# A decoder trunk on one core: the engine that forms the modulation values

## The chip, the core and the metric

The kernel runs on one NeuronCore of a Trainium2 chip. Five engines work beside each other from their own instruction queues: TensorE (PE, matrix products into PSUM), VectorE (DVE), ScalarE (ACT), GpSimd (POOL) and SyncE (SP, which here only issues loads). 16 DMA engines move data between HBM and SBUF. The metric is the device time of one execution in microseconds; lower is better.

## The reference

The program is a trunk of two layers over 256 tokens of 1024 features. Each layer is steered by a conditioning vector `c`:

```python
c_act = silu(c)
for l in range(2):
    mod = (c_act @ ada_w[l] + ada_b[l]).reshape(bsz, 6, 1, 1024)
    shift1, scale1, gate1, shift2, scale2, gate2 = (mod[:, i] for i in range(6))
    h = rmsnorm(x, mix_norm_g[l]) * (1 + scale1) + shift1
    # four mixers of h: S5, sparse attention, RG-LRU, RWKV-7; their gated merge; a projection
    x = x + gate1 * mixed
    h2 = rmsnorm(x, ffn_norm_g[l]) * (1 + scale2) + shift2
    x = x + gate2 * moe(h2, ...)      # 16 experts, 2 of them per token
```

`mod` is a product of one row with a matrix of 1024 x 6144 per layer: little arithmetic, and 25 MB of float32 weights per layer that are read once.

## The kernel before

All weights come in pages of [128, 2048] float32 (1 MB) over SP's queue, in one order that is fixed when the program is built (`order`, line 173 on). A page goes to one of five ring pages; where the state `wide` is set (line 1666, after the mixers), it may also go to one of 15 general pages as long as more than `keep` of them are free (`issue`, `ahead`). A page is given back by `done`, which at once issues the next load that finds room.

The 6144 modulation values of a layer are three groups of 2048 (shift1 and scale1; gate1 and shift2; scale2 and gate2). A group's weights are eight pages, one for each 128 of the 1024 conditioning features; `ada(l, g, kt)` (line 447) takes one of them. Its output are four rows of 512, at partitions 0, 32, 64 and 96. There are two ways:

- Groups (0, 0) and (1, 0), named by `EARLY` (line 26), use PE: per page four matmuls of 32 columns by 512 (line 460), which accumulate in one PSUM bank `acc` over the eight pages. The trace has two records for each float32 matmul. Such a set of four is called a pack here.
- The other four groups use DVE: each page is multiplied by its feature's `csil` and added to a partial sum of [128, 2048] in a general page, in four instructions of 512 columns (line 468; the first page by ACT, line 466). After the eighth page a pack of PE with a matrix of ones sums over the partitions (line 474).

Then both add the bias (line 476), and `mod_values` transposes and stores the values.

Group (0, 0) is needed first and runs at the start, before anything else on PE. The others are among the work of `fill` (line 1262), which lies beside the mixers: `fill_plan` puts two or three pages of modulation weights ahead of each gate product (`feat_steps`, line 614: 48 products of 128 x 128 x 256 per page, in three parts of 12 significant bits that ACT and DVE form, lines 581 and 582). Layer 0 has groups (0, 1), (0, 2) and (1, 0) there, layer 1 has (1, 1) and (1, 2). The main loop steps three chains (RWKV; attention, then S5, then RG-LRU; the tables of S5) in turn, and `fill` by one to three steps for each round of them. This gives the order in which the program is written. The framework then sets, at build time and by its own cost estimate, the order of each engine's queue: an operation that is ready may go ahead of an earlier one that is not. On the chip each engine's order is fixed. Tiles of PSUM have tags with a number of banks: `acc` three, `mx` two, `rw` three.

Of the kernel before, what the change touches and what calls it, by code (L numbers as in the profile page):

```python
"""Hybrid decoder trunk: S5, sparse attention, RG-LRU and RWKV-7 mixers, gated merge, grouped MoE."""
# [13 lines left out]
F32R = mybir.dt.float32r                 # 12 significant bits: a float32 is exactly the sum of two  # L15
AF = mybir.ActivationFunctionType
OP = mybir.AluOpType
# [8 lines left out]
EARLY = [(0, 0), (1, 0)]                 # modulation values by PE instead of DVE: layer, group  # L26
NW = 2                                   # buffers of halves of weights
NR, NM = 5, 15                           # pages of 8 KB per partition: of the weight stream, of everything else
KEEP = 1                                 # pages of the latter that the stream leaves free
FILL, SPARE = (2, 2, 2, 2, 1, 3, 3), 2   # work beside the mixers: steps of it per step of them, pages it leaves free  # L30
XAT, MAT_AT = 3, 3                       # pages of the stream that x and the small matrices follow
PLAN = "1311330100b0322d22ac"            # that work: gates of a branch (0 to 3), its merge (a to d)
PSB = dict(acc=3, mx=2, rw=3)            # banks of PSUM: dense products, small ones, RWKV
TM = (164, 256, 256, 256)                # columns of iq | ik | iw, of q, k and v
# [5 lines left out]
# Columns of the per-feature parameters of a layer: name, number of columns.  # L40
# [9 lines left out]
# Small matrices of a layer, side by side.  # L50
# [27 lines left out]
class Pages:  # L78
    """Pages of [128, 2048] float32 in SBUF, whole or in slots of 512; the longest free goes first."""

    def __init__(self, pool, name, n):
        self.tiles = [pool.tile([P, 2048], F32, tag=f"{name}{i}", name=f"{name}{i}") for i in range(n)]
        self.free_pages = list(range(n))
        self.slots = []                 # free slots of split pages: (page, slot)
        self.used = {}                  # page -> slots in use, of split pages
        self.owner = {}
# [60 lines left out]
def _emit(ctx, tc, I, out):  # L147
# [26 lines left out]
    # ------------------------------------------------------------------ weight stream  # L174
    order, loaded = [], {}
    state = dict(next=0, wide=False)

    def fill_plan(l):
        """What runs beside the mixers: the gates, and modulation values that are needed later."""
        groups = [(l, 1), (l, 2)] + ([(l + 1, 0)] if l + 1 < L else [])  # L180
        adas = [("ada", ll, g, kt) for ll, g in groups for kt in range(KT)]
        plan, k, ng, seen = [], 0, len(groups), [0] * 4
        for c in PLAN:
            if c.isdigit():
                plan += adas[k:k + ng] + [("gate", l, seen[int(c)], int(c))]
                k += ng
                seen[int(c)] += 1
            else:
                plan.append(("br", l, "abcd".index(c)))
        return plan  # L190
# [41 lines left out]
    def ahead():  # L232
        while state["next"] < len(order):
            key = order[state["next"]][0]
            if state["wide"] and key[0] not in ("br", "out", "w13", "w2", "gate", "ada"):
                state["wide"] = False
# [14 lines left out]
    # ------------------------------------------------------------------ inputs and constants  # L251
# [45 lines left out]
    # Masks of 64 x 64 tiles: rows (p mod 64) are s, columns t; t > s, t >= s, and the blocks that  # L297
    # the recursive inverse joins.
# [17 lines left out]
    # Slots of a pair (e, e + 8) of experts: 32..95 and then 0..31 for e, 96..127 and then 0..31 for e + 8.  # L316
# [3 lines left out]
    # Of four, an earlier one (last index) also goes before an equal one.  # L320
# [8 lines left out]
    # ------------------------------------------------------------------ small accurate functions  # L329
# [22 lines left out]
    def sincos(sn, cs, ang, shape):  # L352
        """Reduction by quarter turns in parts that multiply exactly, then polynomials."""
# [26 lines left out]
        half(y, n)                                                       # floor(n / 2)  # L380
        V.scalar_tensor_tensor(m, y, -2.0, n, op0=OP.mult, op1=OP.add)   # n mod 2
        half(n, y)
        V.scalar_tensor_tensor(y, n, -2.0, y, op0=OP.mult, op1=OP.add)
        V.tensor_scalar(y, y, -2.0, 1.0, op0=OP.mult, op1=OP.add)        # sign
# [11 lines left out]
    def exp_acc(o, a, shape):  # L396
        """exp to about a unit in the last place; zero where it underflows."""
# [22 lines left out]
    def log1p_twice(o, q, t, s):  # L420
        """2 log(1 + q) for q in 0..1, by an atanh series."""
        V.tensor_scalar(o, q, 2.0, None, op0=OP.add)
        V.reciprocal(o, o)
        V.tensor_tensor(o, o, q, OP.mult)                                # at most 1 / 3
# [9 lines left out]
    # ------------------------------------------------------------------ conditioning  # L434
# [12 lines left out]
    def ada(l, g, kt):  # L447
        """Of 2048 of the 6144 modulation values, one of 8 parts of the sum; they end in rows
        0, 32, 64, 96 of [128, 512]."""
        early = (l, g) in EARLY  # L450
        if kt == 0:
# [3 lines left out]
            part[l, g] = b, pt("acc", [P, 512]) if early else M.take([P, 2048])  # L455
        b, p = part[l, g]
        w = get(("ada", l, g, kt))
        if early:
            for j in range(4):
                PE.matmul(p[32 * j:32 * j + 32, :], csil[:, kt, :], w[:, 512 * j:512 * j + 512],  # L460
                          start=kt == 0, stop=kt == KT - 1)
        else:
            for j in range(4):
                js = slice(512 * j, 512 * j + 512)
                if kt == 0:
                    S.activation(p[:, js], w[:, js], AF.Copy, scale=csil[:, kt, 0:1])
                else:
                    V.scalar_tensor_tensor(p[:, js], w[:, js], csil[:, kt, 0:1], p[:, js], op0=OP.mult, op1=OP.add)  # L468
        done(("ada", l, g, kt))
        if kt == KT - 1:  # L470
            if not early:
                a, p = p, pt("acc", [P, 512])
                for j in range(4):
                    PE.matmul(p[32 * j:32 * j + 32, :], ones_f[:, 0:32], a[:, 512 * j:512 * j + 512], start=True, stop=True)
                M.free(a)
# [3 lines left out]
    def ada_cols(r):  # L479
        """[128, 4, 4]: value j * 512 + c * 128 + p of the group."""  # L480
# [7 lines left out]
    def ada_rows(o, r, j0):  # L488
        """Half of rows j0, j0 + 1 of the group on every partition, [128, 1024]."""
# [34 lines left out]
    def gate_rows(l, i):  # L524
        """Half of gate i (0 of the mixers, 1 of the experts) on every partition."""
# [6 lines left out]
    # ------------------------------------------------------------------ norm  # L532
# [5 lines left out]
    def rstd(ss, a):  # L538
        """1 / norm of the tokens of a tile."""
# [16 lines left out]
    def modT(x, rs, sc, sh, put):  # L556
        """Feature-major normalised and modulated input: put(k2, p, f) takes blocks 2 k2 and 2 k2 + 1,
        f(kt, o, p) is the modulation of one."""
# [20 lines left out]
    def halves(hi, lo, a):  # L579
        """a is hi + lo, each of 12 bits."""  # L580
# [12 lines left out]
    def hs(h, kt, a=None):  # L593
        """A block of features of the input, of all tokens or of a half."""
        return h[:, T * kt:T * kt + T] if a is None else h[:, T * kt + P * a:T * kt + P * a + P]

    def chunks(key, n):
        """The halves of a page of weights, four blocks of n columns at a time: (kt, hi, lo)."""
# [8 lines left out]
    def three(p, kt, wh, wl, first, last, a=None):  # L607
        """p += weights times input, without the product of the low halves. The first and the last of a bank
        are told: its columns are one group."""
# [8 lines left out]
    def feat_steps(p, key, nb):  # L618
        """nb blocks of 128 features, feature-major: [128, nb, 256]."""
# [15 lines left out]
    # ------------------------------------------------------------------ tables  # L635
# [15 lines left out]
    def prep():  # L651
        sh, s3 = [P, NS], [P, L, 8]
        lre, lim, a, b, sn, cs = (sm(f"s5p{k}", s3, F32, 1) for k in range(6))
        # exponentials of log_step and, for softplus(-lam) = max(-lam, 0) + log(1 + exp(-|lam|)), of -|lam|
# [16 lines left out]
        # (lam_bar - 1) / lam  # L671
# [28 lines left out]
    def s5_tables(l, tabs):  # L700
        """cos and sin of t * theta, [128, 8, 256] each, by doubling."""
# [32 lines left out]
    def others(l, m, tabs, brs):  # L734
        """The other three mixers one after another, their projections first."""
# [13 lines left out]
    # ------------------------------------------------------------------ RWKV-7  # L749
# [11 lines left out]
    def rwkv(l, m, brs):  # L761
# [46 lines left out]
        # decay = exp(-exp(-1/2) sigmoid(z)) = (1 - T) / (1 + T)  # L808
# [13 lines left out]
        # the key's direction, normalised per head  # L822
# [55 lines left out]
        # products of pairs of tokens, transposed: [s, chunk, {t > s, t >= s}, t]  # L878
# [16 lines left out]
        # X = (I + A)^-1 by doubling the block, and Y = X^T  # L895
# [38 lines left out]
        # chunks in turn  # L934
# [41 lines left out]
        # norm over the head  # L976
# [22 lines left out]
    # ------------------------------------------------------------------ sparse attention  # L999
# [23 lines left out]
    def dsa(l, o, brs):  # L1023
# [35 lines left out]
        for a in range(2):  # L1059
            n = P * (a + 1)  # L1060
            ta = slice(P * a, P * a + P)
            # indexer
# [17 lines left out]
            # the 64 largest, the first of equals before the others  # L1080
# [52 lines left out]
    # ------------------------------------------------------------------ S5  # L1133
    def gelu2(o, y):
        """2 * gelu(y)."""
# [8 lines left out]
    def s5(l, u, m, tabs, brs):  # L1144
        cs, sn = tabs
        # C times (lam_bar - 1) / lam
# [15 lines left out]
        for blk in range(2):  # L1162
# [20 lines left out]
            # Re(C s): s_re = cos w_re - sin w_im, s_im = cos w_im + sin w_re  # L1183
# [32 lines left out]
    # ------------------------------------------------------------------ RG-LRU  # L1216
# [574 lines left out]
```

## Time and profile before

| | |
|---|---|
| timed runs | 1261.24, 1261.74, 1262.14 us; median 1261.74 |
| the profiled execution, first to last instruction | 1258.4 us |
| PE busy | 1105.5 us (88%) |
| DVE busy | 752.8 us (60%) |
| ACT busy | 374.1 us (30%) |
| POOL busy | 257.5 us (20%) |
| data read from HBM | 327.19 MB |

The profiled execution's own time is that span; the page gives none beside it. Busy means that at least one instruction of the engine was under way. The ends of matmuls are modelled, so that successive products overlap in the record. The mixers take about 44 to 346 us in layer 0 and 661 to 944 us in layer 1, the experts 400 to 607 and 1000 to 1250 us. A granted clock of 1.00 is 2.4 GHz, and 1.2 GHz is the other level; a value between is the mean over a stretch.

### The profile page before, as it was taken

How to read it: one execution, taken by the hardware profiler on the slowest of the kernel's cores; microseconds unless marked ns; L12 is line 12 of the kernel's file. 1: busy time of each engine (PE TensorE's matmuls, PEld its weight loads, DVE VectorE, ACT ScalarE, POOL GpSimd, SP SyncE). 2: the span in 40 equal slices, each digit the busy share in tenths (PEclk: the TensorE clock that was granted, in tenths of full speed). 3: DMA queues.
4: the chain of work that ended last, by engine and by line, in shares of the span. 5: the costliest groups of instructions: out<-in, count | busy, mean ns of one | idle time of the engine just before them, and what ended most of it. 6: DMA issues, size and time to landing. Idle time of an engine off the chain costs nothing. (4 is left out here: it accounts for less than half of the span.)

```text
span 1258.4 us, 22758 instructions
## 1 busy us (share of the span) xinstructions
PE 1105.5 (88%) x9286; PEld 722.1 (57%) x9286; DVE 752.8 (60%) x1439; ACT 374.1 (30%) x662; POOL 257.5 (20%) x320
## 2 busy tenths in 40 slices
PE   3878999988986999998849899998898699999894
PEld 0878886856873345332218798886677444443321
DVE  5789995598666134232275899959877623233223
ACT  1543433415432111110026544541354211011101
POOL 0593112151232000000091111115414200000000
PEclk8888999989997999998969899999899799999897
DMA  9635787625564999999803468832346489999951
GB/s 357 232 126 208 294 304 292 244 70 199 179 255 150 362 407 421 421 421 410 323 34 134 137 235 299 302 135 101 140 177 255 165 323 416 421 420 420 419 223 52
DMA packets 47089, 329.83 MB, mean 262 GB/s; under 512 B 5992, under 2 KB 6120, under 8 KB 7552
## 3 DMA queue, kind: packets, MB, share of 16 engines
q1 hardware_dynamic: 45776, 327.47, 66.9%
q8 instruction: 78, 1.28, 0.4%
q10 hardware_dynamic: 1200, 0.79, 0.2%
q14 instruction: 35, 0.29, 0.1%
HBM read 327.19 MB, written 1.05 MB: 261 GB/s over the span
## 5 line engine op out<-in xcount | busy, mean ns | idle before, releaser
L614 PE MATMUL acc<-h_hi,whi 128*128 128x256 f32 x720 | 213.8, 297 | 0.2 <-ACT whi L581 0.2
L614 PE MATMUL acc<-h_hi,wlo 128*128 128x256 f32 x720 | 206.3, 287 | 3.5 <-DVE wlo L582 3.5
L614 PE MATMUL acc<-h_lo,whi 128*128 128x256 f32 x720 | 206.4, 287 | 3.3 <-DVE h_lo L582 3.3
L582 DVE TENSOR_TENSOR wlo<-ring,whi 128x1024 fp32r<-128x1024 f32 (+2 forms) x122 | 152.6, 1254 | 62.7 <-ACT whi L581 54.7
L581 ACT ACTIVATE whi<-ring 128x1024 fp32r<-128x1024 f32 (+2 forms) x122 | 125.9, 1033 | 208.9 <-PE acc L614 145.9
L1560 PE MATMUL acc<-page,page 128*32 128x512 f32 (+1 forms) x1408 | 174.3, 600 | 0.0
L614 PEld LDWEIGHTS acc<-h_hi,whi 128*128 128x128 f32 x720 | 138.6, 192 | 16.8 <-issue 7.4
L614 PEld LDWEIGHTS acc<-h_lo,whi 128*128 128x128 f32 x720 | 139.0, 193 | 7.4 <-DVE h_lo L582 4.1
L614 PEld LDWEIGHTS acc<-h_hi,wlo 128*128 128x128 f32 x720 | 139.0, 193 | 6.7 <-DVE wlo L582 4.5
L1560 PEld LDWEIGHTS acc<-page,page 128*32 128x32 f32 x1408 | 48.8, 110 | 95.2 <-issue 90.8
L1591 DVE SCALAR_TENSOR_TENSOR page<-mx,moslw,page 128x512 f32<-128x512 f32 x32 | 24.0, 751 | 124.9 <-PE mx L1584 124.9
L1584 PE MATMUL mx<-page,page 128*32 (+1 forms) x704 | 87.4, 630 | 5.2 <-ACT page L1485 5.2
L1560 PE MATMUL acc<-ring,page 128*32 128x512 f32 (+1 forms) x640 | 84.7, 595 | 0.0
L468 DVE SCALAR_TENSOR_TENSOR page<-ring,csil,page 128x512 f32<-128x512 f32 x112 | 83.0, 780 | 0.0
L1516 POOL TENSOR_TENSOR page<-page,page 128x512 f32<-128x512 f32 x6 | 7.6, 1271 | 328.4 <-DVE page L1515 233.2
L1538 DVE TENSOR_TENSOR page<-page,acc 128x512 f32<-128x512 f32 x64 | 41.7, 683 | 51.9 <-PE acc L1537 51.2
L1474 DVE SCALAR_TENSOR_TENSOR page<-page,acc 128x512 f32<-128x512 f32 x16 | 11.0, 687 | 96.9 <-ACT page L1473 96.9
L1584 PEld LDWEIGHTS mx<-page,page 128*32 128x32 f32 x704 | 24.1, 116 | 59.3 <-issue 49.1
L581 ACT ACTIVATE wlo<-page 128x512 fp32r<-128x512 f32 x32 | 20.2, 631 | 123.5 <-DVE page L1591 123.5
L1473 ACT ACTIVATE page<-acc 128x512 f32<-128x512 f32 x16 | 9.6, 597 | 154.2 <-PE acc L1560 154.2
L1317 POOL TENSOR_TENSOR page<-page,page 128x512 f32<-128x512 f32 x21 | 32.3, 1557 | 79.3 <-DVE page L1315 78.3
L1537 PE MATMUL acc<-wlo,whi 128*128 128x512 f32 x128 | 44.7, 438 | 2.3 <-ACT wlo L581 1.4
(514 smaller groups left out, 2102.8 us busy)
## 6 DMA issues: line engine op xcount, KB each, us to landing
page<-in_w SPq DMA_DIRECT2D x132, 1024.0 KB, 12.1
ring<-in_w SPq DMA_DIRECT2D x60, 1024.0 KB, 11.3
ring<-in_ada_w SPq DMA_DIRECT2D x48, 1024.0 KB, 5.2
ring<-in_gate_w SPq DMA_DIRECT2D x32, 1024.0 KB, 5.8
ring<-in_branch_w SPq DMA_DIRECT2D x8, 1024.0 KB, 4.8
ring<-in_w_rw SPq DMA_DIRECT2D x6, 1024.0 KB, 10.2
ring<-in_w_tm SPq DMA_DIRECT2D x6, 1024.0 KB, 4.8
ring<-in_w_fm SPq DMA_DIRECT2D x6, 1024.0 KB, 4.8
```

The lines of the kernel that those rows point to most:

```text
L468: V.scalar_tensor_tensor(p[:, js], w[:, js], csil[:, kt, 0:1], p[:, js], op0=OP.mult, op1=OP.add)
L581: S.activation(hi, a, AF.Copy)
L582: V.tensor_tensor(lo, a, hi.bitcast(F32), OP.subtract)
L614: PE.matmul(p, w, x_, **f)
L1317: G.tensor_tensor(mix[dp], mix[dp], t, OP.add)
L1473: S.activation(a, h1, AF.Tanh, scale=0.5)
L1474: V.scalar_tensor_tensor(b, a, 1.0, h1, op0=OP.add, op1=OP.mult)
L1537: PE.matmul(p, oh[:, P * a:P * a + P], y[:, fs], start=y is yh, stop=y is yl)
L1538: V.tensor_tensor(x[:, a, fs], x[:, a, fs], p, OP.add)
L1560: PE.matmul(hh[f][32 * g:32 * g + 32, :], xg[:, kt, P * i + 32 * g:P * i + 32 * g + 32], w[:, ds(offs[g] + 512 * f, 512)], start=kt == 0, ...
L1584: PE.matmul(yp[f][32 * g:32 * g + 32, :], gT[:, ft, 32 * g:32 * g + 32], w[:, ds(offs[g] + 512 * f, 512)], start=ft == 0, stop=ft == 3)
L1591: V.scalar_tensor_tensor(t, yp[f], now["w"][:, i:i + 1], gate2[:, fs], op0=OP.mult, op1=OP.mult)
```

## The change

All six groups go the way of `EARLY`: the branch, the partial sum in a general page and the pack with ones are gone, and each group holds one bank of `acc` from its first page to its last. The state `wide` is set from the beginning, with eight general pages kept free, and the load of `x` no longer ends it; so the last three pages of group (0, 0) may go to general pages, until the first weights of RWKV end it. Comments are taken out too, which shifts the line numbers by a few.

```diff
-EARLY = [(0, 0), (1, 0)]
...
-    state = dict(next=0, wide=False)
+    state = dict(next=0, wide=True, keep=8)
...
-            if state["wide"] and key[0] not in ("br", "out", "w13", "w2", "gate", "ada"):
+            if state["wide"] and key[0] not in ("br", "out", "w13", "w2", "gate", "ada", "x"):
                 state["wide"] = False
...
     def ada(l, g, kt):
-        early = (l, g) in EARLY
         if kt == 0:
             b = M.take([P, 512])
             G.memset(b, 0.0)
             nc.scalar.dma_start(b[0:P:32, :], I["ada_b"][l, g])
-            part[l, g] = b, pt("acc", [P, 512]) if early else M.take([P, 2048])
+            part[l, g] = b, pt("acc", [P, 512])
         b, p = part[l, g]
         w = get(("ada", l, g, kt))
-        if early:
-            for j in range(4):
-                PE.matmul(p[32 * j:32 * j + 32, :], csil[:, kt, :], w[:, 512 * j:512 * j + 512],
-                          start=kt == 0, stop=kt == KT - 1)
-        else:
-            for j in range(4):
-                js = slice(512 * j, 512 * j + 512)
-                if kt == 0:
-                    S.activation(p[:, js], w[:, js], AF.Copy, scale=csil[:, kt, 0:1])
-                else:
-                    V.scalar_tensor_tensor(p[:, js], w[:, js], csil[:, kt, 0:1], p[:, js], op0=OP.mult, op1=OP.add)
+        for j in range(4):
+            PE.matmul(p[32 * j:32 * j + 32, :], csil[:, kt, :], w[:, 512 * j:512 * j + 512],
+                      start=kt == 0, stop=kt == KT - 1)
         done(("ada", l, g, kt))
         if kt == KT - 1:
-            if not early:
-                a, p = p, pt("acc", [P, 512])
-                for j in range(4):
-                    PE.matmul(p[32 * j:32 * j + 32, :], ones_f[:, 0:32], a[:, 512 * j:512 * j + 512], start=True, stop=True)
-                M.free(a)
             V.tensor_tensor(b, p, b, OP.add)
             mod_values(l, g, b)
```

## Rows read from the trace of the kernel before

**Rows 1.** The page's part 1: busy us, share of the span, instructions.

```profile
PE 1105.5 (88%) x9286; PEld 722.1 (57%) x9286; DVE 752.8 (60%) x1439; ACT 374.1 (30%) x662; POOL 257.5 (20%) x320
```

**Rows 2.** Windows, layer 0's mixers: length; PE, PEld, DVE, ACT, POOL busy; PE clock; DMA share; GB/s.

```profile
94.00:126.00 32.00, 27.43 (x215) 25.72 (x216) 29.55 (x46) 12.42 (x16) 12.77 (x14) 0.89 0.56 207
126.00:158.00 32.00, 30.71 (x443) 27.03 (x442) 31.31 (x60) 15.39 (x31) 5.83 (x5) 1.00 0.78 294
158.00:189.00 31.00, 29.53 (x478) 26.90 (x477) 29.23 (x53) 11.70 (x27) 3.22 (x2) 1.00 0.84 303
189.00:221.00 32.00, 31.04 (x326) 21.79 (x319) 19.14 (x44) 10.45 (x22) 6.90 (x9) 1.00 0.77 292
...
252.00:284.00 32.00, 29.15 (x172) 19.34 (x173) 31.12 (x47) 3.86 (x6) 16.61 (x17) 0.89 0.23 78
...
sum 252.00, PE 232.78 PEld 194.56 DVE 202.14 ACT 98.59 POOL 62.91; mean PE 29.10 PEld 24.32 DVE 25.27 ACT 12.32 POOL 7.86
```

**Rows 3.** The same windows over layer 1's mixers.

```profile
724.00:755.00 31.00, 31.00 (x351) 28.99 (x351) 28.80 (x42) 13.56 (x23) 5.64 (x5) 1.00 0.66 237
...
787.00:818.00 31.00, 31.00 (x411) 27.81 (x409) 29.62 (x53) 16.27 (x38) 3.36 (x3) 1.00 0.83 307
...
sum 252.00, PE 234.59 PEld 204.18 DVE 212.72 ACT 107.90 POOL 57.19; mean PE 29.32 PEld 25.52 DVE 26.59 ACT 13.49 POOL 7.15
```

**Rows 4.** Line 468: durations in ns, first and last start; its busy time in eight windows.

```profile
L468 DVE SCALAR_TENSOR_TENSOR page<-ring,csil,page x112: 714/741/1695, 109.0 to 809.2; 128x512 f32<-128x512 f32 x112
...
sum 253.00, DVE 83.04; mean DVE 10.38
```

**Rows 5.** Order of time on PE around packs: start us, busy us, operation.

```profile
151.32 1.06 PE L474 MATMUL acc<-page,ones_f 128*32 128x512 f32 x8
152.31 0.39 PE L614 MATMUL acc<-h_hi,whi 128*128 128x256 f32 x1
...
193.65 1.06 PE L460 MATMUL acc<-ring,csil 128*32 128x512 f32 x8
...
204.65 2.78 PE L460 MATMUL acc<-ring,csil 128*32 128x512 f32 x24
207.36 0.38 PE L614 MATMUL acc<-h_hi,whi 128*128 128x256 f32 x1
207.58 0.28 PE L614 MATMUL acc<-h_lo,whi 128*128 128x256 f32 x1
```

**Rows 6.** PE's holes: one in order of time; then waits, 246 to 346 us (total, times, longest).

```profile
97.72 1.12 PE L842 MATMUL rw<-identr,page 128*128 128x128 f32 x4 [4.77 <-DVE page L837]
...
PEld mx L1186 <- POOL page L1179: 7.1, 4, 2.9
...
PE mx L1186 <- DVE page L1178: 5.6, 3, 2.7
```

**Rows 7.** The start: a wait of PE, loads that SP issues, windows as in rows 2.

```profile
PE acc L460 <- DMA ring<-in_ada_w: 5.8, 4, 3.2
...
8.24 9.74 SPq L228 DMA_DIRECT2D ring<-in_ada_w  x4
...
0.00:8.00 8.00, 0.00 (x0) 0.00 (x0) 2.71 (x32) 1.49 (x2) 2.40 (x17) 1.00 0.60 177
8.00:16.00 8.00, 3.27 (x16) 0.80 (x20) 7.69 (x73) 0.00 (x0) 0.00 (x0) 1.00 0.99 408
...
24.00:32.00 8.00, 5.74 (x25) 0.75 (x26) 1.82 (x6) 1.04 (x2) 0.00 (x0) 0.59 1.02 422
```

**Rows 8.** Order of time on DVE: the search's rounds with and without sums.

```profile
149.02 0.28 DVE L1083 MAX8 dsm<-page 128x8 f32<-128x128 f32 x1
...
150.79 0.28 DVE L1083 MAX8 dsm<-page 128x8 f32<-128x128 f32 x1
...
202.34 0.43 DVE L1083 MAX8 dsm<-page 128x8 f32<-128x256 f32 x1
...
203.32 0.43 DVE L1083 MAX8 dsm<-page 128x8 f32<-128x256 f32 x1
```

## The prediction

> **What bounds the kernel now.** I read the page's busy line first, then a table of equal windows over the two mixer stretches, then the waits of TensorE (PE) in them, then the order of time around the operations that the change moves. The busy line puts PE at 1105.5 of 1258.4 us and VectorE (DVE) at 752.8 [rows 1]: PE is the busiest engine over the whole, but that is a mean over stages. The table is the view that decides. Where the modulation sums run on DVE, in layer 0 from 109.0 us on [rows 4] and in layer 1 up to 809, both engines look full: DVE 31.31 of 32 and 29.23 of 31 us, PE 30.71 of 32 and 29.53 of 31 [rows 2], and in layer 1 PE 31.00 of 31 [rows 3]. So which of the two sets the pace? Three things say PE. In the window right behind, 189 to 221, DVE has no such sums and falls to 19.14 of 32, yet PE stays at 31.04 of 32 at full clock [rows 2]: freeing DVE did not free PE. Between 85 and 252 us PE has only one long wait, 4.77 us on L837, and it ends at 97.72 us [rows 6], before the first sum on DVE. And what DVE does in the sums is filler: no instruction is listed as waiting for L468, and only the end of a group has a reader. So in these stretches PE works through a list that is always full, and DVE is full beside it because it was given filler.
>
> **The change part by part.**
>
> *Added on PE.* Four groups of eight pages, so 32 packs of four matmuls of 32 columns each. Group (1, 0) already runs this way beside the mixers of layer 0, so the price is measured in place: three packs take 2.78 us, 0.93 each, and one alone 1.06 [rows 5]. I take 0.93: 32 x 0.93 = 29.8 us, and 33.9 at the upper end.
>
> *Removed from PE.* Each of the four groups ended with a pack that summed over partitions (L474). It begins at 151.32 and the next product at 152.31 [rows 5]: 0.99 us, so 4 x 0.99 = 4.0 us. Net on PE: +25.8 us.
>
> *Removed from DVE and ACT.* 112 instructions of L468, 83.0 us of DVE [rows 4], and eight activations a layer on ACT, which is far from full. I cost this at nothing: PE covers it, since PE does not wait there for DVE. If that cover were not there it would be worth up to 83 us; the first rival below is about that.
>
> *What PE's holes give back.* PE is idle 252.0 - 232.8 = 19.2 us between 94 and 346 and 252.0 - 234.6 = 17.4 us between 692 and 944 [rows 2, 3]. The 4.77 us hole at L837 can take packs if their pages are there: three, 2.8 us. The other large holes belong to the S5 mixer (7.1 and 5.6 us on L1179 and L1178 [rows 6]); PE's order is fixed when the program is built and it stands in that order behind a product that waits, so more filler does not fill them by itself. I take 4 us for all others in both layers together. Ends: nothing, or all 36.6.
>
> *Tile shape.* A pack works in 32 columns between products of 128. The first product after three packs took 0.38 us, the next 0.28 [rows 5]: 0.10 us for the way back. Many packs stand beside 64-column products of RWKV, which change the shape anyway, so I take 0; the upper end is 32 x 0.10 = 3.2 us. The Trainium skill, TensorEngine Tiling (Array Packing), Key Properties, says that changing the tiling mode drains TensorE; this is the rule that speaks against the change. The trace agrees with it by those 0.10 us; counted on the way in and the way out, 64 x 0.10 = 6.4 us, it would make the forecast 1287 instead of 1281.
>
> *The bank.* A group now keeps one of three accumulator banks for its eight pages, and products of the gates have two. Group (1, 0) does that in 189 to 221, and PE is idle 0.96 us there [rows 2], no more than beside it. I take 0; the upper end is that whole idle time for each of four groups, 3.8 us. The first pack of a group waits for a free bank and the fill's later products stand behind it on PE, until ACT has read one of the gates' banks.
>
> *Big pages at first.* The last three pages of group (0, 0) go to the general pages at once instead of waiting for ring pages. But the DMA engines are busy 0.99 to 1.02 of the time in the windows from 8 to 32 us [rows 7], of which the first and the last of three are shown: the bytes that come before the last of these pages are the same, so it lands no sooner. The first 8 us have idle DMA time, but there the issue of later pages was behind (the fifth page goes out at 8.24 us [rows 7]) while ring pages were free. What could be gained is that gap, (1 - 0.60) x 8 = 3.2 us [rows 7]; what could be lost, by small loads that come later behind more large ones, I bound by the 3.2 us longest wait of PE for a modulation page [rows 7]. I take 0. On the queue of SyncE the weights of RWKV stay behind the eight pages and x, in the same order; on GpSimd and ACT the clearing and the bias load of a group stay where they are.
>
> *Pages.* A group no longer holds a page of 8 KB per partition for its partial sums, so the stream and the fill may find a page sooner; with PE full that is worth 0, and the bound is within the holes above.
>
> *Sum.* 25.8 - 2.8 - 4 = +19 us on the profiled execution: 1258.4 to about 1277.4. The timed runs have their median at 1261.74, 3.3 us over that span, which I leave as it is: 1261.7 + 19 = **1281**. What is late next is everything behind the packs on PE: the mixers' products, then the merge, the output projection, and the expert stage, which starts that much later in each layer and has its own load stream tied to the same pages.
>
> **The rivals.**
>
> *DVE was the limiter (faster).* Mechanism: the mixers' chains wait on DVE's in-order queue behind the sums. The top-64 search shows it: in layer 0 its rounds begin at 149.02 and 150.79, 1.77 us apart with sums between, and at 202.34 and 203.32, 0.98 apart without, although each step is longer there [rows 8]. Chains that end earlier let S5 start earlier and leave more gate products to lie beside it. Against it: PE was not waiting for those chains. Price: it decides from the point where more than 25.8 of PE's 36.6 idle us come back; if all do, -10.8, that is **1251**. The Trainium skill, Perfetto Trace Analysis, Identifying the Most-Contended Engine, says that matmul busy time is no good measure for TensorE and that the busy share of weight loads is better. By that, PE is 27.03 / 32 = 84% and 26.90 / 31 = 87% full where I call it full [rows 2], and this rival has more room than I give it; that no wait is seen there keeps me with the other.
>
> *It comes out even.* The holes, the cold clock (0.89 granted in 94 to 126 and in 252 to 284 [rows 2], so 3.5 us lost in each, PE being less busy there) and the earlier chains return just about the 25.8: **1262**.
>
> *Dearer.* Packs at 1.06, the way back at 0.10, the bank's 3.8, no hole filled: 33.9 - 4.0 + 3.2 + 3.8 = +36.9, **1299**.
>
> *It does not do what it says.* The big pages may never matter, since the ring is not what limits the start; that is my value for that part, and it changes nothing in the sum.
>
> **How the numbers follow.** PE-bound with part of the holes, 0.60: between +13 (another 6 us of holes back) and +27 (no hole filled, a little for the way back), 1275 to 1289, likeliest 1281. DVE the limiter, 0.18, 1251. Even, 0.09. Dearer, 0.13. Runs of this kernel lie within 0.9 us, and 0.2% (2.5 us) is about what can be told from no change. Faster is the second case, 0.18; same the third, 0.09; slower the first and the fourth, 0.73. The range must take in the even case, a part of the faster one and the lower part of the dearer one: 1256 to 1292.
>
> **What would show it.** Right: the packs of L460 are three times as many as before, DVE busy falls by about 80 us, and PE busy rises by 20 to 28 us; in the windows that hold the packs PE stays above 95% while DVE falls towards 60%; the start of layer 0's expert stage and of layer 1 move later by about 10 us each; the last pack of group (0, 0) begins within 1 us of where it did. Wrong: PE's busy time rises but the stretch of mixers gets shorter, with S5 starting earlier; or PE shows waits on the loads of modulation pages or on the reading of a bank; or the first product of layer 0 comes some us earlier.

## The result, and the profile after

The changed kernel takes 1275.92 us (median of 4 runs, 1272.37 to 1279.4) where the kernel before took 1261.49 (4 runs, 1257.71 to 1262.14): the ratio is 1.0119 with a 95% interval of 1.0091 to 1.0148. It is slower by about 14 us; the forecast was 1281, 19 over before. The profiled execution has a span of 1273.4 us against 1258.4, 15.0 more.

Lines behind the modulation code have moved: L460 of before is L457, L614 is L599, L842 is L827, L1083 is L1068, L1483 is L1468, L1560 is L1545, L1576 is L1561 and L1584 is L1569.

The page's part 1 and its group of the packs from ring pages (instructions, busy us, mean ns), and then, from the view of that line, the packs that read general pages:

```profile
PE 1129.7 (89%) x9510; PEld 729.8 (57%) x9510; DVE 678.2 (53%) x1327; ACT 364.5 (29%) x646; POOL 250.6 (20%) x320
...
L457 PE MATMUL acc<-ring,csil 128*32 128x512 f32 x360 | 47.0, 618 | 16.5 <-DVE csil L439 12.6
```

```profile
L457 PE MATMUL acc<-page,csil x24: 1061/1062/1063, 24.1 to 30.1; 128*32 128x512 f32 x24
```

PE is 24.2 us busier than in [rows 1], DVE 74.6 less busy, and there are 360 + 24 = 384 records of packs, three times 128.

The windows of layer 0's mixers, with the columns of [rows 2]:

```profile
126.00:158.00 32.00, 32.00 (x440) 25.18 (x443) 14.29 (x38) 11.81 (x27) 4.94 (x6) 1.00 0.72 280
158.00:189.00 31.00, 30.59 (x446) 23.15 (x440) 12.33 (x19) 10.29 (x24) 1.22 (x2) 1.00 0.73 281
189.00:221.00 32.00, 31.31 (x333) 22.18 (x329) 17.16 (x38) 9.40 (x19) 5.67 (x8) 1.00 0.72 280
221.00:252.00 31.00, 31.00 (x335) 25.67 (x336) 13.36 (x26) 13.27 (x31) 0.29 (x1) 1.00 0.71 281
```

From 126 to 189 us DVE has fallen from 60.54 us [rows 2] to 26.62, less than half of the 63 us. PE is as full as it was and passes fewer instructions: 886 matmul records where it passed 921. That is the whole case in two numbers: the engine that was relieved was not the one that set the pace.

Where the 15.0 us arise is read from four marks, the starts of single operations in the order of time on PE: the first product of the RWKV norm and the first of the expert stage, in each layer. Of before:

```profile
400.41 1.08 PE L1560 MATMUL acc<-page,page 128*32 x4
...
711.93 0.60 PE L842 MATMUL rw<-identr,page 128*128 128x128 f32 x4
...
1005.19 1.08 PE L1560 MATMUL acc<-page,page 128*32 x4
```

(its first mark, 97.72, is in [rows 6]), and of the changed kernel:

```profile
99.28 1.12 PE L827 MATMUL rw<-identr,page 128*128 128x128 f32 x4 [3.60 <-DVE page L822]
...
413.00 1.08 PE L1545 MATMUL acc<-page,page 128*32 x4
...
721.12 0.60 PE L827 MATMUL rw<-identr,page 128*128 128x128 f32 x4
...
1024.42 1.08 PE L1545 MATMUL acc<-page,page 128*32 x4
```

The marks are later by 1.6, 12.6, 9.2 and 19.2 us. So the mixers of layer 0 take 11.0 us more and those of layer 1 take 10.0 more. That is 21.0 + 1.6, more than the 15.0 of the whole: some 4 us are given back in each layer between the expert stage's first product and its end. All of that lies in the last expert step, where a branch is (`tc.If` around `dense`, L1576 of before). PE in order of time, before:

```profile
623.48 1.90 PE L1560 MATMUL acc<-ring,page 128*32 x16
628.27 1.09 PE L1483 MATMUL rw<-identr,page 128*128 128x128 f32 x4 [2.89 <-PEq L1576]
630.10 4.49 PE L1584 MATMUL mx<-page,page 128*32 x20 [0.74 <-ACT page L1485]
...
1227.88 1.90 PE L1560 MATMUL acc<-ring,page 128*32 x16
1233.68 1.01 PE L1483 MATMUL rw<-identr,page 128*128 128x128 f32 x4 [3.90 <-issue]
1235.42 3.63 PE L1584 MATMUL mx<-ring,page 128*32 x16 [0.74 <-ACT page L1485]
```

and after:

```profile
639.98 0.63 PE L1468 MATMUL rw<-identr,page 128*128 128x128 f32 x4 [1.70 <-DVEq L1561]
641.34 4.93 PE L1569 MATMUL mx<-page,page 128*32 x44 [0.74 <-ACT page L1470]
...
1250.74 0.63 PE L1468 MATMUL rw<-identr,page 128*128 128x128 f32 x4 [1.72 <-DVEq L1561]
1252.10 1.92 PE L1569 MATMUL mx<-ring,page 128*32 x16 [0.74 <-ACT page L1470]
```

Before, PE stands 2.89 and 3.90 us at the branch, and behind it 20 records of L1584 take 4.49 us; after, it stands 1.70 and 1.72, and 44 records of the same line take 4.93. Windows that hold the end of the hole and what comes behind it, of before and then of after, show why (the granted clock is third from the end):

```profile
626.00:632.00 6.00, 2.99 (x16) 1.31 (x20) 0.69 (x1) 0.60 (x1) 3.47 (x20) 0.66 0.36 117
...
1231.00:1237.00 6.00, 2.58 (x12) 1.14 (x16) 0.09 (x1) 0.60 (x1) 0.00 (x0) 0.59 0.27 91
```

```profile
639.00:645.00 6.00, 4.29 (x40) 1.62 (x44) 1.07 (x2) 0.60 (x1) 4.62 (x26) 1.00 0.39 116
...
1250.00:1256.00 6.00, 4.53 (x42) 1.63 (x46) 0.34 (x1) 0.60 (x1) 0.00 (x0) 1.00 0.26 91
```

The granted clock fell to 0.66 and 0.59 behind the longer holes and stayed at 1.00 behind the shorter ones. From the last SwiGLU of the stage to the reading of its result it is 13.5 and 13.8 us before, 9.5 and 9.5 after.

### The profile page after: what moved, and what is told of

Same layout as the page of the kernel before. It is cut to its first block, busy times and chain, and to the rows that moved or that the text cites. A ratio compares the mean times of both kernels' runs of the same rounds, so it can differ in the third digit from the quotient of the medians.

```text
span 1273.4 us, 23072 instructions
## 1 busy us (share of the span) xinstructions
PE 1129.7 (89%) x9510; PEld 729.8 (57%) x9510; DVE 678.2 (53%) x1327; ACT 364.5 (29%) x646; POOL 250.6 (20%) x320
## 5 line engine op out<-in xcount | busy, mean ns | idle before, releaser
L599 PE MATMUL acc<-h_hi,whi 128*128 128x256 f32 x720 | 215.9, 300 | 0.7 <-ACT whi L566 0.7
L599 PE MATMUL acc<-h_lo,whi 128*128 128x256 f32 x720 | 207.6, 288 | 3.4 <-DVE h_lo L567 3.4
L599 PE MATMUL acc<-h_hi,wlo 128*128 128x256 f32 x720 | 207.7, 288 | 2.8 <-DVE wlo L567 2.8
L1545 PE MATMUL acc<-page,page 128*32 128x512 f32 (+1 forms) x1408 | 174.3, 600 | 0.0
L599 PEld LDWEIGHTS acc<-h_hi,whi 128*128 128x128 f32 x720 | 140.6, 195 | 18.5 <-issue 9.3
L599 PEld LDWEIGHTS acc<-h_lo,whi 128*128 128x128 f32 x720 | 140.6, 195 | 8.0 <-DVE h_lo L567 4.3
L599 PEld LDWEIGHTS acc<-h_hi,wlo 128*128 128x128 f32 x720 | 140.8, 196 | 5.6 <-DVE wlo L567 3.7
L1545 PEld LDWEIGHTS acc<-page,page 128*32 128x32 f32 x1408 | 48.8, 110 | 95.2 <-issue 90.1
L1569 PE MATMUL mx<-page,page 128*32 (+1 forms) x704 | 85.2, 616 | 5.2 <-ACT page L1470 5.2
L1576 DVE SCALAR_TENSOR_TENSOR page<-mx,moslw,page 128x512 f32<-128x512 f32 x32 | 24.0, 751 | 120.3 <-PE mx L1569 120.3
L1545 PE MATMUL acc<-ring,page 128*32 128x512 f32 (+1 forms) x640 | 84.7, 595 | 0.0
L457 PE MATMUL acc<-ring,csil 128*32 128x512 f32 x360 | 47.0, 618 | 16.5 <-DVE csil L439 12.6
L1569 PEld LDWEIGHTS mx<-page,page 128*32 128x32 f32 x704 | 23.8, 113 | 56.4 <-issue 46.4
## 6 DMA issues: line engine op xcount, KB each, us to landing
page<-in_w SPq DMA_DIRECT2D x132, 1024.0 KB, 13.5
```

The source lines that it names most:

```text
L599: PE.matmul(p, w, x_, **f)
L1545: PE.matmul(hh[f][32 * g:32 * g + 32, :], xg[:, kt, P * i + 32 * g:P * i + 32 * g + 32], w[:, ds(offs[g] + 512 * f, 512)], start=kt == 0, ...
L1569: PE.matmul(yp[f][32 * g:32 * g + 32, :], gT[:, ft, 32 * g:32 * g + 32], w[:, ds(offs[g] + 512 * f, 512)], start=ft == 0, stop=ft == 3)
L1576: V.scalar_tensor_tensor(t, yp[f], now["w"][:, i:i + 1], gate2[:, fs], op0=OP.mult, op1=OP.mult)
```

## The experiments

My theory: PE's packs are the cost, and nothing else in the change counts. The first rival: VectorE limits, and something in the change hides what its relief brings. For each run the table below gives the two mixer stretches (from the RWKV norm's first product to the expert stage's first product) and the last expert step, besides the time; a single trace says little about 3 to 5 us, as kernels with the same mixer code differ by that much (layer 1's stretch, the same in "fewer packs" and in the kernel before, was 296.4 and 293.3; in "shift changed" it was 307.6, in three others with its mixers 303.0 to 304.3).

| | median us | ratio to before (95%) | mixers L0, L1 | last step L0, L1 |
|---|---|---|---|---|
| before | 1260 to 1261 | | 302.7, 293.3 | 13.5, 13.8 |
| changed | 1275.92 | 1.0119 (1.0091-1.0148) | 313.7, 303.3 | 9.5, 9.5 |
| packs only | 1275.48 | 1.0110 (1.0065-1.0156) | 315.4, 303.0 | 13.7, 9.6 |
| pages only | 1257.92 | 1.0003 (0.9975-1.0031) | 300.7, 293.3 | 9.8, 14.0 |
| no sums | 1257.77 | 0.9984 (0.9955-1.0013) | 300.2, 293.3 | 13.6, 13.5 |
| sums beside | 1279.89 | 1.0148 (1.0088-1.0209) | 314.3, 304.3 | 13.8, 9.7 |
| two packs | 1253.63 | 0.9945 (0.9920-0.9971) | 302.9, 293.4 | 13.6, 9.9 |
| double packs | 1309.03 | 1.0384 (1.0335-1.0434) | 336.2, 316.1 | 13.7, 9.7 |
| held bank | 1262.01 | 1.0005 (0.9978-1.0032) | 305.0, 296.3 | 13.5, 9.4 |
| fewer packs | 1260.59 | 0.9994 (0.9959-1.0030) | 305.9, 296.4 | 15.5, 9.3 |
| shift before | 1252.42 | 0.9936 (0.9904-0.9968) | 304.5, 293.0 | 11.0, 10.1 |
| shift changed | 1279.46 | 1.0140 (1.0064-1.0216) | 313.3, 307.6 | 13.3, 13.7 |
| GpSimd sums | 1270.42 | 1.0093 (1.0055-1.0131) | 317.6, 293.1 | 14.0, 9.3 |

**Packs only**: the kernel before, every group by PE.

```diff
-EARLY = [(0, 0), (1, 0)]
+EARLY = [(l_, g_) for l_ in range(2) for g_ in range(3)]
```

> Only the packs: all six groups on TensorE, the load stream as before. If the packs are the whole cause (theory): the first products of S5 come 11 to 13 us later in layer 0 and the mixers of layer 1 lose another 10 to 12, as in the changed kernel; 1270 to 1280 us, the spread being the last step of each expert stage. If the big pages have a part (rival), it differs from the changed kernel's 1276 by more than 4 us in the stretch before 126 us.

Measured 1275.48: the packs alone make the whole loss.

**Pages only**: the kernel before with the stream's state of the change.

```diff
-state = dict(next=0, wide=False)
+state = dict(next=0, wide=True, keep=8)
...
-            if state["wide"] and key[0] not in ("br", "out", "w13", "w2", "gate", "ada"):
+            if state["wide"] and key[0] not in ("br", "out", "w13", "w2", "gate", "ada", "x"):
```

> Only the load stream: general pages for the first modulation weights. Theory: 1258 to 1264 us, and no gain at the start, since the loads are saturated from 8 to 40 us; the RWKV norm on TensorE perhaps 1.6 us later, as in the changed kernel. Rival: a gain of 2 us or more at the start that the packs hid.

Level, 1.0003. The last four packs of group (0, 0) in order of time on PE:

```profile
21.95 1.07 PE L460 MATMUL acc<-ring,csil 128*32 128x512 f32 x8 [3.80 <-DMA ring<-in_ada_w]
24.44 1.94 PE L460 MATMUL acc<-page,csil 128*32 128x512 f32 x8 [1.42 <-DMA page<-in_ada_w]
27.03 1.94 PE L460 MATMUL acc<-page,csil 128*32 128x512 f32 x8 [0.66 <-DMA page<-in_ada_w]
29.51 1.93 PE L460 MATMUL acc<-page,csil 128*32 128x512 f32 x8 [0.55 <-DMA page<-in_ada_w]
```

Three pages did go to general pages and came 2.5 us apart as they do from the ring; the last pack begins at 29.51, in the kernel before at 29.22 and in the changed one at 29.21.

**No sums**: the kernel before without the 112 sums.

```diff
+                if kt:
+                    continue
                 if kt == 0:
```

> The kernel before without the sums on VectorE: of the four groups only the first page is used, so 112 instructions (83 us of VectorE) are gone and TensorE has the same work. If TensorE sets the pace (theory): 1254 to 1262 us, S5 in layer 0 starts within 3 us of where it did. If VectorE sets it in those stretches (rival): 20 us or more faster, below 1242.

0.9984 with 1 in its interval: 83 us of DVE [rows 4] taken away are worth nothing that can be told. Its windows:

```profile
126.00:158.00 32.00, 30.39 (x440) 26.74 (x439) 17.68 (x43) 13.07 (x27) 5.33 (x6) 1.00 0.72 269
158.00:189.00 31.00, 31.00 (x475) 27.26 (x475) 13.74 (x20) 13.78 (x29) 2.88 (x3) 1.00 0.74 297
189.00:221.00 32.00, 32.00 (x336) 23.36 (x336) 18.70 (x46) 8.61 (x19) 5.09 (x8) 1.00 0.76 290
```

DVE is at 31.42 of 63 us where it was at 60.54 [rows 2], and PE passes 915 records where it passed 921. This settles the rival.

**Sums beside**: the changed kernel, and the old sums too, into a page that nobody reads.

```diff
+        if (l, g) not in ((0, 0), (1, 0)):
+            if kt == 0:
+                late[l, g] = M.take([P, 2048])
+            for j in range(4):
+                js, q = slice(512 * j, 512 * j + 512), late[l, g]
+                if kt == 0:
+                    S.activation(q[:, js], w[:, js], AF.Copy, scale=csil[:, kt, 0:1])
+                else:
+                    V.scalar_tensor_tensor(q[:, js], w[:, js], csil[:, kt, 0:1], q[:, js], op0=OP.mult, op1=OP.add)
+            if kt == KT - 1:
+                M.free(q)
```

> The changed kernel with the old sums on VectorE and ScalarE as well, into a page that nobody reads: TensorE as in the changed kernel, VectorE as in the one before. Theory: within 4 us of the changed kernel, 1272 to 1280. Rival, that a freed VectorE gave part of the packs' cost back: 8 us or more slower, above 1284.

1279.89, 4 over the changed kernel with intervals that overlap, and mixers 0.6 and 1.0 us longer: DVE can carry its old load beside the packs at almost no cost.

**Two packs**: the changed kernel, 24 of 32 late packs left out.

```diff
+            if (l, g) in ((0, 0), (1, 0)) or kt in (0, KT - 1):
                 PE.matmul(p[32 * j:32 * j + 32, :], ...)
```

> The changed kernel, but of each of the four late groups only pages 0 and 7 get a pack: 24 of its 32 late packs, six eighths of the sums of those groups, are left out, while bank, stream, ending and DVE's relief stay as changed. Theory (TensorE is what ends the mixers, each pack pushes it): the mixers get shorter by 24 x 0.75 to 24 x 0.93 us, 18 to 22 us under the changed kernel's 1276, so 1254 to 1258; the stretch from layer 1's RWKV norm to the first product of its expert stage falls from 303 to 291 to 295 us. Rival (the price hangs on the group: its bank, its place in the order, its ending): it stays above 1268.

1253.63, 22.3 under the changed kernel: 0.93 a pack. By the traces the mixers are 10.8 and 9.9 us shorter for 12 packs each, 0.90 and 0.83.

**Double packs**: the changed kernel, each pack twice.

```diff
+        for r in range(2):
             for j in range(4):
-                PE.matmul(..., start=kt == 0, stop=kt == KT - 1)
+                PE.matmul(..., start=kt + r == 0, stop=kt + r == KT)
```

> The changed kernel with every pack of all six groups issued twice into the same sums (the factor halved, so that the values are the same): 32 late and 8 packs of group (1,0) more beside the mixers; those of group (0,0) lie under the first loads. Theory (each pack has its price wherever it stands): 40 x 0.75 to 40 x 0.93 us more, 30 to 37 over 1276: 1306 to 1313. Rival (the price is the change of tile shape at a pack and back, not the passes): a pack beside a pack is nearly free, under 10 us more, below 1286.

1309.03, 33.1 over the changed kernel: 0.83 for each of 40 packs. A pack directly behind a pack costs nearly as much as one by itself, so the price is in the four passes; of a single pack's 0.93, some 0.1 us at most is left for the change of shape. The prediction weighed a rule of the Trainium skill here (TensorEngine Tiling (Array Packing), Key Properties: a change of tiling mode drains TensorE); the trace does not contradict the rule, but what a drain costs beyond that does not show in these 40 packs.

**Held bank**: the kernel before, a late group holds its bank from its first page.

```diff
+            if not early:
+                held[l, g] = pt("acc", [P, 512])
...
+        if kt == 0 and not early:
+            PE.matmul(held[l, g][0:32, 0:16], csil[:, 0, :], w[:, 0:16], start=True, stop=True)
...
-                a, p = p, pt("acc", [P, 512])
+                a, p = p, held[l, g]
```

> The kernel before, but each of the four late groups takes its bank of sums with its first page (one matmul of 16 columns opens it) and keeps it to its end, as the changed kernel does; VectorE forms the values as before. Theory (the bank held longer holds nobody up): 1258 to 1266, level with before; its priced upper end was 3.8 us, so at most 1264 or so from 1260. Rival (the bank is a good part of the 15 us): 1268 or more.

Level, 1.0005, though its trace has a last step in layer 1 that is 4.4 us shorter than before, as in all kernels whose code lies otherwise there (below). The mixers of its trace are 2.3 and 3.0 us longer, no more than unchanged code varies (3.1 in layer 1 of "fewer packs"), so by this run alone a price of up to some 5 us for the bank is neither shown nor excluded; a good part of the 15 us it is not. "Two packs" speaks against a price: its four late groups hold their banks as in the changed kernel, and with eight late packs in place of four packs with ones its mixers take 302.9 and 293.4 us, where three traces with the mixers of before have 302.6 and 293.2 on the mean.

**Fewer packs**: the kernel before, one group more on DVE.

```diff
-EARLY = [(0, 0), (1, 0)]
+EARLY = [(0, 0)]
```

> The kernel before one step the other way: group (1,0), too, is formed by VectorE, so that 8 packs leave layer 0's mixers, one pack with ones and 28 sums of 0.74 us (20.8 us) of VectorE come in. Theory (TensorE ends the mixers, VectorE has room): 8 x 0.75 to 8 x 0.93 less 1.0 us, 5 to 6.5 us under the kernel before, 1253.5 to 1255; from layer 0's RWKV norm to its expert stage 296 to 298 us where it took 302.7. Rival (VectorE limits the mixers as much): 1262 or more.

A miss: 1260.59 where I expected 1253.5 to 1255. Layer 0's mixers did not become 5 us shorter but 3.2 longer. The window where the packs of (1, 0) had been:

```profile
189.00:221.00 32.00, 27.27 (x248) 23.18 (x246) 27.03 (x59) 9.89 (x21) 1.80 (x2) 0.84 0.73 279
```

DVE went from 19.14 us [rows 2] to 27.03, and PE fell from 31.04 to 27.27 busy at a granted clock of 0.84. Of PE's waits from 97 to 346 us (total, times, longest) that for DVE's low part of the weights was, before,

```profile
PE acc L614 <- DVE wlo L582: 2.4, 3, 1.1
```

and with the group on DVE

```profile
PE acc L614 <- DVE wlo L582: 4.7, 5, 1.8
```

So PE's 7 us of work that went away came back as idle time: over layer 0's whole stretch PE is idle 37.2 us where it was 30.3 (305.8 - 268.7 and 302.7 - 272.4). The 3.2 us by which the stretch is longer are within what unchanged code varies; that the gain did not come is not. In this place, unlike that of the late groups, nothing is to be won by going back to DVE. That DVE is the limit there is argued and not shown: the waits for its low part give 2.3 of the 7 us, the rest is spread over other waits. (The whole stayed at 1260.59 with a short last step in layer 1, below.)

**GpSimd sums**: the same step, but the group's products on ACT and its sums on GpSimd.

```diff
+                if kt and (l, g) == (1, 0):
+                    t = M.take([P, 512])
+                    S.activation(t, w[:, js], AF.Copy, scale=csil[:, kt, 0:1])
+                    G.tensor_tensor(p[:, js], p[:, js], t, OP.add)
+                    M.free(t)
```

> The kernel before, but group (1,0) leaves TensorE (8 packs less, one pack with ones more) for ScalarE and GpSimd: 28 products of 128x512 on ScalarE (about 0.6 us each, 17 us) and 28 sums on GpSimd (1.3 to 1.6 us each, 36 to 45 us), which has 10 of 63 us of work from 189 to 252; its values are not needed before layer 1. VectorE's load stays as before, unlike in the run where VectorE took that group and nothing was won. Theory (TensorE and VectorE are level in layer 0's mixers, so a pack comes free only if VectorE takes nothing for it): 8 x 0.83 to 0.93 less 1.0, 5.5 to 6.5 us under the kernel before, 1253.5 to 1255. Rival (the packs of (1,0) are free where they stand, or ScalarE comes to wait behind GpSimd for the four quarter pages of products): 1259 or more.

1270.42, the rival's side. A wait of ACT from 97 to 346 us, then a window of before and the same of this run:

```profile
ACT page L467 <- POOL page L468: 21.3, 18, 3.1
```

```profile
221.00:252.00 31.00, 29.80 (x273) 25.28 (x271) 16.75 (x28) 13.45 (x30) 3.29 (x4) 1.00 0.62 241
```

```profile
221.00:252.00 31.00, 24.43 (x220) 18.24 (x221) 11.47 (x17) 14.68 (x31) 14.81 (x15) 0.83 0.38 138
```

ACT stood 21.3 us behind GpSimd's sums before it could write the next product. Such a page of modulation weights keeps its ring page until then: in the window the DMA engines are busy 0.38 where the kernel before has 0.62 and PE 24.43 us where it has 29.80, and layer 0's mixers took 14.9 us more. So this does not test whether TensorE and VectorE are level there; its carriers were too slow.

**Shift before and shift changed**: the last expert step. Tiny matmuls under the first loads move all later code of PE and change nothing else.

```diff
+    pad = pt("mx", [P, 16])
+    for i in range(SHIFT):                   # 111 in the kernel before, 33 in the changed one
+        PE.matmul(pad, ones_b, ones_b[:, 0:16], start=i == 0, stop=i == SHIFT - 1)
```

> The kernel before with 111 tiny matmuls (16 columns, bf16) at the very start, under the first loads, into a bank that nobody reads: they push all later code of TensorE by 222 instructions; nothing else changes. The last step of each expert stage has so far taken 9.3 to 9.9 us where TensorE's hole at the branch was 2.1 to 2.7 us, and 13.5 to 15.5 us where it was 3.5 us or more. In layer 1 the hole was 4.5 to 4.8 us in all three kernels whose code lies as in the kernel before, and 2.1 to 2.7 in the seven others. Theory (in layer 1 the place of the code sets the hole): layer 1's hole falls from 4.5 to 2.1 to 2.7 us and its last step from 13.8 to 9.3 to 9.9; the whole 1254 to 1260. Rival (chance of each execution): the hole stays at 3.5 or more and the step at 13.5 or more. Layer 0's was long and short with the same code, so neither says anything of it.

> The changed kernel with 33 such tiny matmuls at the very start: they put layer 1's branch at the same place in a 16 KB block of TensorE's code as in the kernel before (16 KB is the size of one instruction load in the trace, 256 instructions if one is 64 bytes). Theory (the place of the code sets the hole in layer 1): layer 1's hole grows from 2.3 to 4.5 us or so, its last step from 9.5 to 13.5 to 14; the whole about 4 over the changed kernel's 1276, 1276 to 1284. Rival (chance, or the place has nothing to do with it): step 9.3 to 9.9, the whole 1272 to 1280.

Layer 1's branch on PE, first of shift before, then of shift changed (the lines lie four further down than in the kernel that each starts from):

```profile
1223.98 1.90 PE L1564 MATMUL acc<-ring,page 128*32 x16
1227.34 0.63 PE L1487 MATMUL rw<-identr,page 128*128 128x128 f32 x4 [1.47 <-DVE page L1479]
```

```profile
1252.21 1.90 PE L1549 MATMUL acc<-ring,page 128*32 x16
1258.43 0.63 PE L1472 MATMUL rw<-identr,page 128*128 128x128 f32 x4 [4.32 <-issue]
```

Both holes went as the theory said: the kernel before lost its long one (3.90 to 1.47 us idle, last step 13.8 to 10.1) and the changed kernel got it (1.72 to 4.32, 9.5 to 13.7). The changed kernel's time rose by 3.5 us, about the 4 expected, but its four runs spread over 17 us. "Shift before" took 1252.42 us, less than the 1254 to 1260 expected, and beats both kernels without a change in what is computed. Not all of its 8 us is explained: in its trace the last step of layer 1 gives 3.7, and 3.1 come from two earlier expert steps of layer 1 that are some 1.6 us shorter each. Such steps of 1.6 us are in most of the traces here, with and without a shift; their cause is open. Its layer 0 ends where it did before (638.8 and 638.7).

## Why the prediction was right

- **The pace is PE's: right.** Both tests of it agree: without its sums DVE gave nothing back (no sums), and with its old load beside the packs it cost almost nothing (sums beside). That holds for the late groups. A rule of the Trainium skill (Perfetto Trace Analysis, Identifying the Most-Contended Engine: the busy share of weight loads tells more than that of matmuls) spoke for the other side with 84% and 87%. In this case the matmul row was the better guide: at that weight-load share there was nothing to win.
- **The rival's observation was true and did not matter.** The search's rounds in layer 0, which had been 1.77 us apart beside the sums [rows 8], are 0.72 apart in the changed kernel:

```profile
151.72 0.29 DVE L1068 MAX8 dsm<-page 128x8 f32<-128x128 f32 x1 [0.40 <-POOL page L1063]
152.44 0.29 DVE L1068 MAX8 dsm<-page 128x8 f32<-128x128 f32 x1
153.15 0.30 DVE L1068 MAX8 dsm<-page 128x8 f32<-128x128 f32 x1
...
213.20 0.43 DVE L1068 MAX8 dsm<-page 128x8 f32<-128x256 f32 x1 [0.87 <-POOL page L1063]
```

  The search is faster where it is on DVE, but the next one has its first round only at 213.20, while in the kernel before it was under way at 202.34 [rows 8]. Between the two PE is full (windows above), with packs among its products.
- **The price of a pack, 0.93: right on PE.** In the changed kernel's order of time two late packs take 1.85 us to the next product, 0.93 each:

```profile
130.79 1.92 PE L457 MATMUL acc<-ring,csil 128*32 128x512 f32 x16
132.64 1.15 PE L743 MATMUL rw<-identr,page 64*64 64x64 f32 x32
```

  What a pack adds to the time is 0.83 when doubled and 0.93 when taken out. Four traces have all 32 late packs (changed, packs only, sums beside, shift changed): their mixers take 314.2 and 304.6 us on the mean. Three have the mixers of before (before, pages only, shift before): 302.6 and 293.2. The difference is 11.5 + 11.4 = 22.9 us for 32 packs less four packs with ones; with 4.0 us for the latter, as predicted, that is 26.9 / 32 = 0.84 a pack.
- **What holes give back: the term that was mis-sized.** I took 2.8 + 4 = 6.8 us off the 25.8 and had 19.0 for the mixers; they lost 22.9, so 2.9 came back. (These 2.9 are also the whole distance from 0.93 to 0.84 a pack: it is one amount, not two.) PE's records do not show that even these came out of holes: over both stretches PE is busy 560.4 us on the mean of the four traces and 536.7 on that of the three, some 24 more, and idle 58.3 where it was 59.2 (55.6 to 60.6 in the four, 58.0 to 61.0 in the three). The 2.8 at L837 did not come: the hole is still there (3.60 us at 99.28, shown above), and the first late pack begins at 130.79.
- **Bank, way back, big pages, freed page: nothing, as taken.** For the big pages this is shown (pages only). For the packs' change of shape it is shown within 0.1 us a pack. "Sums beside" takes pages as before for its sums, and its mixers differ from the changed kernel's by 0.6 and 1.0 us. For the bank "two packs" shows no price, within the 3 to 5 us that a trace is good for.
- **What the sum did not have: the last expert step.** By the mixers alone I should have said +23 and been further off. The new code lies differently: in layer 1 this is shown by the two shifts and takes off some 4 us. In layer 0 the same code had a long hole in one execution and a short one in another (before 13.5 and pages only 9.8; changed 9.5 and packs only 13.7), so the 4.0 us that its profile gives back there are of that execution and say nothing of the change. That leaves 22.9 - 4.3 = 18.6 us where 14.4 were measured: the interval of the ratio reaches from 11.5 to 18.7 us, and the rest is open. So the mechanism was right, but that the forecast came so near is in part luck: holes too generous by about 4 us, and 4 us of code placement the other way that no row read before could have foretold.
- **The spread of runs was taken too small.** The 0.9 us came from three runs; 58 later ones of the kernel before lie between 1251.44 and 1266.68.
- **What was to be seen**: packs three times as many, PE +24.2, DVE -74.6, expert stage of layer 0 and start of layer 1 later by 12.6 and 9.2, last pack of (0, 0) at 29.21 against 29.22: all as said. Only DVE went lower than the 60% I named, to 45% and 40%.

## What to carry to other kernels

Where two engines look equally full, ask which of them has a reader waiting; work that nobody waits for soon (here sums whose values are needed much later) can make its engine look full at no cost. Here taking it off that engine gave nothing, and putting it on the other one cost nearly its full price. Take the price from such work in place (0.83 to 0.93 us a pack here, with a neighbour, alone, or left out), and don't expect fixed-order queues to fill holes by themselves. Moving the code alone was worth 0.6% here, so differences of that size between two kernels with different code should be tried with the code moved before they are put down to the edit.

## What the runs showed of the hardware

At the branch behind the experts' products PE stands still, and the trace has 16 KB loads of instructions at that time (of the queue that the page lists as q8, instruction; in layer 0 of before one at 623.78 us took 1.5 us and one at 624.12 took 2.0). In 26 last steps (13 traces, two layers) the first transpose began 2.1 to 2.7 us after the last product in 12, and 3.5 to 5.2 us after it in the other 14. Behind all 14 the granted clock fell (its mean was 0.50 to 0.57 from 1.5 to 4.5 us after the transposes' start, 1.2 GHz or little over), and the step took 13.3 to 15.5 us; behind 11 of the 12 it stayed at 1.00 and the step took 9.3 to 10.1 (in the twelfth, layer 0 of "shift before", it fell for less time, and the step took 11.0). So some 2 us of a hole cost 4. In layer 1 the long hole was in just the four kernels whose first record at the branch is number 2 to 4 of a block of 256, when all of PE's records are counted from its first, weight loads and the sequencer's too (before, pages only, no sums, and shift changed, which was moved there), and in none of the nine others. In layer 0, 10 of 13 were long without such an order.

The loads of instructions tell the two kinds of hole apart, in both layers. Layer 1's hole, of before (1229.2 to 1233.6 us) and of the changed kernel (1248.5 to 1250.7), by queue: packets, MB, share of 16 engines:

```profile
q14 instruction: 2, 0.02, 2.1%
q8 instruction: 1, 0.02, 1.4%
```

```profile
q14 instruction: 1, 0.01, 1.3%
```

In each of the 26 steps the transposes begin 1.2 to 2.5 us after the end of the last 16 KB load of q8 that began before them. Counted from the start of the last product, that load ended after 0.2 to 0.9 us in the 12 short holes and after 1.2 to 3.4 in the 14 long ones. In the four of layer 1 it is one more load, begun 2.3 us after the last product, which in the other nine begins only behind the transposes' start. In layer 0 it is a load begun as late (four of 10) or one that shared its time with another and took 1.9 to 2.1 us where most take about 1 (six). So a long hole goes with code that comes late. That it is the wait for this code is the likely reading, and the two shifts fit it; why loads of layer 0 are late in one execution and not in another is open.
